# A gather, cumulative sum and product on one core: gathers that convert to fp16 as they land, into 64 slots, in place of a cast on ScalarE

## The chip, the core and the metric

One core of a Trainium2 chip runs the whole program. The metric is device time in microseconds (us) of one execution; the numbers quoted are medians of several executions. A ratio is computed as the mean time of one kernel's fast runs over that of the other's fast runs of the same rounds on the same chip, so it is not quite the ratio of the medians that stand beside it. All times are of the core's own clock, without the host.

Engines: PE is TensorE's matmul, PEld its weight load, DVE is VectorE, ACT is ScalarE, POOL is GpSimd, SP is SyncE. The 16 DMA engines are shared by all queues; q0 carries the gathers, which GpSimd issues, and q1 the stores, which SyncE issues.

## The reference

```python
B, S, N, D = (16, 4096, 2048, 512)      # x: [B, S, D] fp32; indices: sorted, N different ones of S; w: [D, D]
gathered = x[b_idx, indices, :]         # 16 x 2048 rows of 2 KB
cs = np.cumsum(gathered, axis=1)
return np.matmul(cs, w)                 # [16, 2048, 512] fp32
```

In tiles of 128 rows there are T = 256 tiles, 16 to a batch. Each tile is 256 KB of x read and 256 KB of output written, 134 MB in all.

## The kernel before

A tile is gathered, cast to fp16, summed down its rows by four matmuls with a triangle of ones, given the carry of the tile ahead on VectorE, multiplied by w in four matmuls, drained by ScalarE and stored. Two tiles are a pair (R = 2): partition p holds rows 2p and 2p+1 of the pair, so a store writes 4 KB in a row.

```python
NG = 16; FAR = 10; NH = 8; NO = 8       # gather slots, how far casts lead, fp16 pairs, output pairs
g32 = [const.tile([P, R, D], FP32) for i in range(NG // R)]
g16 = [const.tile([P, R, D], FP16) for i in range(NH)]

def gather(t):                          # GpSimd
    g, r = divmod(t, R)
    if t >= NG:
        pool.need(s_c, cast_by[R * (g + 1) - NG - 1])       # the slot has been cast
    ...
    nc.gpsimd.indirect_dma_start(out=g32[g % (NG // R)][:, r, :], in_=x_flat,
        in_offset=bass.IndirectOffsetOnAxis(ap=ap, axis=0), ...).then_inc(s_g[t % NG], 16)

def cast(t, n, first=None):             # ScalarE, in turn with the drains
    ...
    nc.scalar.copy(out=g16[g % NH][:, r : r + n],
                   in_=g32[g % (NG // R)][:, r : r + n]).then_inc(s_c, 1)

def sums(t, u, first=None):             # TensorE
    pe.need(s_c, ...)                   # cast
    ...
def drain(u, first=None):               # ScalarE
    nc.scalar.copy(out=ob[g % NO][:, j], in_=pb[u % NB][:]).then_inc(s_e, 1)

def store(g):                           # SyncE, 512 KB
    nc.sync.dma_start(out=rows.rearrange("(p j) d -> p j d", j=R), in_=ob[g % NO][:])

# order on TensorE: sums lead products by
lead = min(LEAD, 1 + (u + 2) // 4, 1 + (T - 1 - u) // 6)
```

Of the kernel before, what the change touches and what calls it, by code (L numbers as in the profile page):

```python
# [33 lines left out]
def kernel(  # L34
# [19 lines left out]
    FIRST = 2 * R  # L54
    NG = 16
    LEAD = 4
    FAR = 10
    NH = 8
    NA = 4
    NB = 4  # L60
    NC = 4
    NO = 8
    U = NT
    assert U % NG == 0 and U % (R * NO) == 0 and U % NA == 0 and U % (R * NC) == 0 and U % NB == 0
    assert D == 512 and N % (R * P) == 0 and T % P == 0
# [16 lines left out]
    spare = const.tile([P, 1], FP16)  # L82
    g32 = [const.tile([P, R, D], FP32, name=f"g32_{i}") for i in range(NG // R)]
    g16 = [const.tile([P, R, D], FP16, name=f"g16_{i}") for i in range(NH)]
    cst = [const.tile([P, DC, R, P], FP16, name=f"cst{i}") for i in range(NC)]
    ob = [const.tile([P, R, D], FP32, name=f"ob{i}") for i in range(NO)]
    pa = [ps.tile([P, DC, R, Q], FP32, name=f"pa{i}") for i in range(NA)]
# [12 lines left out]
    s_idx = [sem(f"s_idx{k}") for k in range(KI)]  # L100
    s_el = [sem(f"s_el{j}") for j in range(R)]
    s_ol = [sem(f"s_ol{j}") for j in range(R)]
    s_g = [sem(f"s_g{i}") for i in range(NG)]
    s_o = [sem(f"s_o{i}") for i in range(NO)]
# [8 lines left out]

    casts = []
    cast_by = []
    for u in range(T):
        far = min(FAR, 2 + u // 4, 2 + (T - 1 - u) // 4)
        casts.append([])
        while len(cast_by) <= min(u + far, T - 1):
            n = R if far > 4 and len(cast_by) % R == 0 else 1  # L120
            casts[u].append((len(cast_by), n))
            cast_by += [cast_by[-1] + 1 if cast_by else 1] * n

    for u in range(3 * U, T - 2 * U):
        assert casts[u] == [(t + U, n) for t, n in casts[u - U]]

    def gather(t):
        g, r = divmod(t, R)
        if t >= NG:
            pool.need(s_c, cast_by[R * (g + 1) - NG - 1])  # L130
        if t < FIRST:
            pool.need(s_first[g], 16)
            ap = idx_first[:, t, 0:1]
        else:
            pool.need(s_prep, t // P + 1)
            ap = idxg[:, t // P, t % P : t % P + 1]
        nc.gpsimd.indirect_dma_start(  # L137
            out=g32[g % (NG // R)][:, r, :],
            out_offset=None,
            in_=x_flat,  # L140
            in_offset=bass.IndirectOffsetOnAxis(ap=ap, axis=0),
            element_offset=(t // NT) * S * D,
        ).then_inc(s_g[t % NG], 16)


    PLAIN = (0, G - 1)

    def cast(t, n, first=None):
        g, r = divmod(t, R)
        for u in range(t, t + n):  # L150
            act.need(s_g[u % NG], 16 * (u // NG + 1), first)
        nc.scalar.copy(  # L152
            out=g16[g % NH][:, r : r + n], in_=g32[g % (NG // R)][:, r : r + n]
        ).then_inc(s_c, 1)

    def sums(t, u, first=None):
        g, r = divmod(t, R)
        tiles = None if first is None else R * first
        pe.need(s_c, cast_by[t] if first is None else cast_by[2 * U + t] - 2 * U // R, first)
        pe.need(s_d, t - NA + 1, tiles)  # L160
        for c in range(DC):
            if c == 1 and u is not None:
                pe.need(s_e, u - NB + 1, tiles)
            mm = nc.tensor.matmul(  # L164
                out=pa[t % NA][:, c],
                lhsT=g16[g % NH][:, r, c * P : (c + 1) * P],
                rhs=uq[:] if first is None and g in PLAIN else ut[:],
                start=(c == 0),
                stop=(c == DC - 1),
            )  # L170
        mm.then_inc(s_a, 1)
# [28 lines left out]
    def project(u, t, first=None):  # L200
        g, j = divmod(u, R)
        tiles = None if first is None else R * first
        pe.need(s_e, u - NB + 1, tiles)
        pe.need(s_d, u + 1 if first is None and g in PLAIN else R * (g + 1), tiles)
        for c in range(DC):
            if c == 2 and t is not None:
                pe.need(s_d, t - NA + 1, tiles)
            mm = nc.tensor.matmul(  # L208
                out=pb[u % NB][:],
                lhsT=cst[g % NC][:, c, j, :],  # L210
                rhs=w16[:, c, :],
                start=(c == 0),
                stop=(c == DC - 1),
            )
        mm.then_inc(s_b, 1)

    def drain(u, first=None):
        g, j = divmod(u, R)
        act.need(s_b, u + 1, first)
        nc.scalar.copy(out=ob[g % NO][:, j], in_=pb[u % NB][:]).then_inc(s_e, 1)  # L220

    def store(g):
        b, h = divmod(g, GB)
        rows = out[b, h * R * P : (h + 1) * R * P, :]
        if g in PLAIN:
            for j in range(R):
                sp.need(s_e, R * g + j + 1)
                done = s_ol[j] if g else (s_o[0], s_of)[j]
                nc.sync.dma_start(
                    out=rows[j * P : (j + 1) * P, :], in_=ob[g % NO][:, j]  # L230
                ).then_inc(done, 16)
            return
        sp.need(s_e, R * (g + 1))
        nc.sync.dma_start(
            out=rows.rearrange("(p j) d -> p j d", j=R), in_=ob[g % NO][:]
        ).then_inc(s_o[g % NO], 16)

# [15 lines left out]
    for c in range(DC):  # L253
        eng = (nc.sync, nc.scalar)[c % 2]
        eng.dma_start(out=w32[:, c, :], in_=w[c * P : (c + 1) * P, :]).then_inc(s_w[c], 16)
    for g in range(G):
        store(g)
    for g in range(G - NO, G - 1):
        sp.need(s_o[g % NO], 16 * (g // NO + 1))
    for j in range(R):  # L260
        sp.need(s_ol[j], 16)

# [77 lines left out]
    for u in range(T):  # L340
        lead = min(LEAD, 1 + (u + 2) // 4, 1 + (T - 1 - u) // 6)
        first = u if u // R in PLAIN else u // R * R + R - 1
# [6 lines left out]
    tail = order.index((False, T - 2 * U - 1)) + 1  # L349
    step = 2 * U  # L350
    for i in range(head + step, tail):
        assert order[i] == (order[i - step][0], order[i - step][1] + U)

    def run(i, first=None):
        is_sums, t = order[i]
        after = next((v for k, v in order[i + 1 :] if k != is_sums), None)
        if first is not None:
            t -= 2 * U
            after -= 2 * U
        if is_sums:  # L360
# [5 lines left out]
    for i in range(head):  # L366
        run(i)
    with nc.tensor.Fori(2 * U // R, (T - 2 * U) // R, U // R) as first:
        pe.new_pass()
# [11 lines left out]
    def step(u, first=None):  # L381
        if u % R == 0:
            if first is None and u == R * NO:
                act.need(s_of, 16)
            act.need(s_o[u // R % NO], 16 * (u // R // NO), first)
        for t, n in casts[u if first is None else 2 * U + u]:
            cast(t if first is None else t - 2 * U, n, first)
        drain(u, first)
# [40 lines left out]
```

## Time and profile before

| | before |
|---|---|
| time, median of 3 | 353.58 us (353.39 to 354.66) |
| span of its first profile | 447.5 us, granted clock 0.88 |
| GpSimd's gathers | 256, one every 1.25 us at best |
| bytes moved | 135.7 MB |

The page lists groups of instructions with their count, busy time, the mean ns of one, and the idle time ahead of them with what ended most of it. The lines that matter are shown in the prediction. The span of this first profile is 27% longer than the timed runs.

### The profile page before, as it was taken

What the parts mean: (1) busy time and instruction counts of PE and PEld (TensorE: products, weight loads), DVE (VectorE), ACT (ScalarE), POOL (GpSimd) and SP (SyncE); (2) the same over time, 40 slices, a digit from 0 to 9 for tenths busy, and PEclk for the clock granted to TensorE, in tenths of its full rate; (3) what the DMA queues carried; (4) which work ended last, traced back from release to release, by engine and by line L of the source; (5) the groups of instructions that cost most, each with busy time, mean ns of one, the idle gap of its engine ahead of it and who ended that gap; (6) DMA issues with size and microseconds to landing.
All of it is one profiled execution on the core that took longest, in us unless ns stands there. A gap on an engine that the chain in (4) does not pass through costs nothing.

```text
span 447.5 us, 6498 instructions
## 1 busy us (share of the span) xinstructions
PE 340.6 (76%) x2066; PEld 170.5 (38%) x2066; DVE 178.5 (40%) x263; ACT 259.6 (58%) x399; POOL 243.9 (54%) x266
## 2 busy tenths in 40 slices
PE   6354687578858887868788877987588888787995
PEld 2111244244424443424344434444244444344552
DVE  3103344224423454443345433444334444343652
ACT  3212467356636676655567655676456666555984
POOL 6771466575556555655656555655556655555300
PEclk9756789796999698988989889889889889799999
DMA  7874589897899888999989899988898988899974
GB/s 231 255 237 146 187 273 338 312 323 264 311 339 322 298 320 313 343 330 325 326 307 346 313 349 325 327 307 302 334 321 316 333 315 299 313 353 332 336 320 187
DMA packets 40619, 135.69 MB, mean 303 GB/s; under 512 B 6816, under 2 KB 7072, under 8 KB 40608
## 3 DMA queue, kind: packets, MB, share of 16 engines
q0 software_dynamic: 20480, 67.13, 47.3%
q1 hardware_dynamic: 19568, 67.91, 37.7%
q10 hardware_dynamic: 560, 0.53, 0.4%
q8 instruction: 5, 0.08, 0.1%
q14 instruction: 6, 0.05, 0.0%
HBM read 68.42 MB, written 67.11 MB: 303 GB/s over the span
## 4 chain that ended last, share of the span: by engine, by line
PE 70%; issue 12%; another core or an unknown queue 7%; ACT 6%; DVE 3%; DMA 1%; POOL 0%; ACTq 0%; DVEq 0%; SPq 0%
PE pb L208 54%; PE pa L164 16%; ACT g L152 3%; ACT ob L220 3%; DVE cst L196 3%; DMA g<-in_x_dram,idx_first 1%; DMA idx_first<-in_indices_dram 0%; DVE cst L183 0%; POOL g L137 0%; ACTq L26 0%; DVEq L26 0%; ACTq L393 0%; SPq L424 0%; SPq L90 0%
## 5 line engine op out<-in xcount | busy, mean ns | idle before, releaser
L137 POOL DMA_INDIRECT g<-in_x_dram,idxg x252 | 238.4, 946 | 173.1 <-ACT g L152 106.4
L208 PE MATMUL pb<-w,cst 128*128 128x512 f16 x1024 | 297.7, 417 | 44.0 <-issue 21.8
L196 DVE TENSOR_TENSOR cst<-pa,cst 128x512 f16<-128x512 f32 x240 | 166.0, 692 | 241.3 <-PE pa L164 152.4
L220 ACT COPY ob<-pb 128x512 f32<-128x512 f32 x256 | 144.9, 598 | 178.2 <-PE pb L208 118.8
L164 PE MATMUL pa<-ut,g 128*128 128x128 f16 x1008 | 113.1, 233 | 55.0 <-issue 21.3
L208 PEld LDWEIGHTS pb<-w,cst 128*128 128x128 f16 x1024 | 95.2, 106 | 126.2 <-issue 48.0
L152 ACT CAST g<-g 128x1024 f16<-128x1024 f32 (+1 forms) x139 | 138.0, 994 | 0.8 <-DMA g<-in_x_dram,idx_first 0.8
L164 PEld LDWEIGHTS pa<-ut,g 128*128 128x128 f16 x1008 | 81.5, 105 | 137.5 <-issue 45.5
L183 DVE CAST cst<-pa 128x512 f16<-128x512 f32 x16 | 11.0, 688 | 15.6 <-PE pa L164 14.0
L304 PE MATMUL pb<-zeros 128*128 128x512 f16 x16 | 5.7, 521 | 1.5 <-DVE zeros L308 1.5
L137 POOL DMA_INDIRECT g<-in_x_dram,idx_first x4 | 4.0, 994 | 1.6 <-issue 0.9
L304 PEld LDWEIGHTS pb<-zeros 128*128 128x128 f16 x16 | 1.9, 127 | 4.0 <-issue 1.9
L164 PE MATMUL pa<-uq,g 128*128 128x128 f16 x16 | 1.6, 220 | 1.7 <-ACT g L152 0.9
L377 ACT ACT_TABLE_LOAD x1 | 1.3, 1283 | 2.5 <-issue 2.5
L380 ACT CAST w<-w 128x512 f16<-128x512 f32 x2 | 1.1, 614 | 2.7 <-DMA w<-in_w_dram 2.7
L311 DVE CAST idxf<-idx 128x128 f32<-128x128 uint32 x2 | 0.5, 264 | 4.2 <-DMA idx<-in_indices_dram 4.2
L164 PEld LDWEIGHTS pa<-uq,g 128*128 128x128 f16 x16 | 1.0, 97 | 3.0 <-ACT g L152 1.5
L325 DVE CAST w<-w 128x512 f16<-128x512 f32 x2 | 0.8, 424 | 1.2 <-DMA w<-in_w_dram 1.2
L316 PE MATMUL pb<-ident,idxf 128*128 128x128 f32 x2 | 0.8, 376 | 0.5 <-DVE idxf L311 0.5
L316 PEld LDWEIGHTS pb<-ident,idxf 128*128 128x128 f32 x2 | 0.4, 186 | 1.4 <-DVE idxf L311 1.1
L308 DVE MEMSET zeros<- 128x256 uint32 x1 | 0.3, 272 | 1.1 <-SPq L90 1.1
L322 DVE CAST idxg<-pb 128x128 uint32<-128x128 f32 x2 | 0.6, 286 | 0.2 <-issue 0.2
(11 smaller groups left out, 2.1 us busy)
## 6 DMA issues: line engine op xcount, KB each, us to landing
out_dram<-ob SPq DMA_DIRECT2D x126, 512.0 KB
g<-in_x_dram,idxg POOLq DMA_INDIRECT x252
out_dram<-ob SPq DMA_DIRECT2D x4, 256.0 KB, 2.0
w<-in_w_dram ACTq DMA_DIRECT2D x2, 256.0 KB
w<-in_w_dram SPq DMA_DIRECT2D x2, 256.0 KB
idx<-in_indices_dram SPq DMA_DIRECT2D x2, 128.0 KB, 2.7
g<-in_x_dram,idx_first POOLq DMA_INDIRECT x4
idx_first<-in_indices_dram ACTq DMA_DIRECT2D x1, 2.0 KB, 2.1
```

The source lines that it names most:

```text
L137: nc.gpsimd.indirect_dma_start(out=g32[g % (NG // R)][:, r, :], out_offset=None, in_=x_flat, in_offset=bass.IndirectOffsetOnAxis(ap=ap, ax ...
L152: nc.scalar.copy(out=g16[g % NH][:, r : r + n], in_=g32[g % (NG // R)][:, r : r + n]).then_inc(s_c, 1)
L164: mm = nc.tensor.matmul(out=pa[t % NA][:, c], lhsT=g16[g % NH][:, r, c * P : (c + 1) * P], rhs=uq[:] if first is None and g in PLAIN else ...
L183: nc.vector.tensor_copy(out=dst, in_=src).then_inc(s_d, 1)
L196: nc.vector.tensor_tensor(out=dst, in0=src, in1=last, op=mybir.AluOpType.add).then_inc(s_d, 1)
L208: mm = nc.tensor.matmul(out=pb[u % NB][:], lhsT=cst[g % NC][:, c, j, :], rhs=w16[:, c, :], start=(c == 0), stop=(c == DC - 1),)
L220: nc.scalar.copy(out=ob[g % NO][:, j], in_=pb[u % NB][:]).then_inc(s_e, 1)
L304: nc.tensor.matmul(out=pb[NB - 1][:], lhsT=zeros[:, :P], rhs=zeros[:], start=True, stop=True)
L316: nc.tensor.transpose(out=pb[k % NB][:, :P], in_=idxf[:, k, :], identity=ident[:]).then_inc(s_pt, 1)
L325: nc.vector.tensor_copy(out=w16[:, c, :], in_=w32[:, c, :]).then_inc(s_wc, 1)
L377: nc.scalar.copy(out=spare[:], in_=zeros[:, :1])
L380: nc.scalar.copy(out=w16[:, c, :], in_=w32[:, c, :]).then_inc(s_wc, 1)
```

## The change

The intent: ScalarE is freed of 138 us of casts, a slot is no longer held until ScalarE comes round to it, gathers can run far ahead of the sums, and half as many bytes are written into on-chip memory by the gathers. The core of the diff:

```diff
-    NG = 16
+    NG = 64        # slots
+    FLY = 16       # gathers under way at most
+    NS = 32
+    FREE = 8
-    FAR = 10
-    NH = 8
-    NO = 8
+    W = 2          # pairs to a store
+    NO = 4
-    g32 = [const.tile([P, R, D], FP32, name=f"g32_{i}") for i in range(NG // R)]
-    g16 = [const.tile([P, R, D], FP16, name=f"g16_{i}") for i in range(NH)]
+    g16 = [const.tile([P, R, D], FP16, name=f"g16_{i}") for i in range(NG // R)]
     def gather(t):
-        if t >= NG:
-            pool.need(s_c, cast_by[R * (g + 1) - NG - 1])
+        if t % FREE == 0:
+            pool.need(s_a, t + FREE - NG)                                # summed
+        if t >= FLY:
+            pool.need(s_g[(t - FLY) % NS], 16 * ((t - FLY) // NS + 1))   # 16 earlier has landed
         nc.gpsimd.indirect_dma_start(
-            out=g32[g % (NG // R)][:, r, :],
+            out=g16[g % (NG // R)][:, r, :],
-    def cast(t, n, first=None):      # ... gone, and its place in ScalarE's order
     def sums(t, u, first=None):
-        pe.need(s_c, ...)
+        pe.need(s_g[t % NS], ...)
-    def store(g):
+    def store(g, n):                 # n pairs, 1 MB for n = 2
-        lead = min(LEAD, 1 + (u + 2) // 4, 1 + (T - 1 - u) // 6)
+        lead = min(LEAD, 1 if u < 2 else 2 + (u + 4) // 12, (T - 1 - u) // 2)
 # ... cut: semaphores, TensorE's loop of 64 tiles in place of 16, the ends of the stores
```

More of the change, by code (lines that the diff above doesn't have):

```diff
@@ L61 @@
     NC = 4
-    NO = 8
+    W = 2
+    NO = 4
     U = NT
-    assert U % NG == 0 and U % (R * NO) == 0 and U % NA == 0 and U % (R * NC) == 0 and U % NB == 0
+    V = NG
+    assert V % NS == 0 and NS == 16 * R and 2 * U % NS == 0 and (T - 4 * U) % V == 0 and U % (W * R * NO) == 0 and U % NA == 0 and U % (R * NC) == 0 and U % NB == 0
     assert D == 512 and N % (R * P) == 0 and T % P == 0
@@ L82 @@
     spare = const.tile([P, 1], FP16)
-    g32 = [const.tile([P, R, D], FP32, name=f"g32_{i}") for i in range(NG // R)]
-    g16 = [const.tile([P, R, D], FP16, name=f"g16_{i}") for i in range(NH)]
+    g16 = [const.tile([P, R, D], FP16, name=f"g16_{i}") for i in range(NG // R)]
     cst = [const.tile([P, DC, R, P], FP16, name=f"cst{i}") for i in range(NC)]
-    ob = [const.tile([P, R, D], FP32, name=f"ob{i}") for i in range(NO)]
+    ob = [const.tile([P, W, R, D], FP32, name=f"ob{i}") for i in range(NO)]
     pa = [ps.tile([P, DC, R, Q], FP32, name=f"pa{i}") for i in range(NA)]
@@ L100 @@
     s_idx = [sem(f"s_idx{k}") for k in range(KI)]
-    s_el = [sem(f"s_el{j}") for j in range(R)]
-    s_ol = [sem(f"s_ol{j}") for j in range(R)]
-    s_g = [sem(f"s_g{i}") for i in range(NG)]
+    s_ol = sem("s_ol")
+    s_g = [sem(f"s_g{i}") for i in range(NS)]
     s_o = [sem(f"s_o{i}") for i in range(NO)]
@@ L112 @@
     )
-    casts = []
-    cast_by = []
-    for u in range(T):
-        far = min(FAR, 2 + u // 4, 2 + (T - 1 - u) // 4)
-        casts.append([])
-        while len(cast_by) <= min(u + far, T - 1):
-            n = R if far > 4 and len(cast_by) % R == 0 else 1
-            casts[u].append((len(cast_by), n))
-            cast_by += [cast_by[-1] + 1 if cast_by else 1] * n
-    for u in range(3 * U, T - 2 * U):
-        assert casts[u] == [(t + U, n) for t, n in casts[u - U]]
     def gather(t):
         g, r = divmod(t, R)
-        if t >= NG:
-            pool.need(s_c, cast_by[R * (g + 1) - NG - 1])
+        if t % FREE == 0:
+            pool.need(s_a, t + FREE - NG)
+        if t >= FLY:
+            pool.need(s_g[(t - FLY) % NS], 16 * ((t - FLY) // NS + 1))
         if t < FIRST:
@@ L142, in gather @@
             element_offset=(t // NT) * S * D,
-        ).then_inc(s_g[t % NG], 16)
+        ).then_inc(s_g[t % NS], 16)
     PLAIN = (0, G - 1)
-    def cast(t, n, first=None):
-        g, r = divmod(t, R)
-        for u in range(t, t + n):
-            act.need(s_g[u % NG], 16 * (u // NG + 1), first)
-        nc.scalar.copy(
-            out=g16[g % NH][:, r : r + n], in_=g32[g % (NG // R)][:, r : r + n]
-        ).then_inc(s_c, 1)
     def sums(t, u, first=None):
@@ L158, in sums @@
         tiles = None if first is None else R * first
-        pe.need(s_c, cast_by[t] if first is None else cast_by[2 * U + t] - 2 * U // R, first)
-        pe.need(s_d, t - NA + 1, tiles)
+        skip = 0 if first is None else 2 * U
+        pe.need(s_g[t % NS], 16 * (t // NS + 1) - skip // R, first)
+        pe.need(s_d, t - NA + 1 - skip, tiles)
         for c in range(DC):
             if c == 1 and u is not None:
-                pe.need(s_e, u - NB + 1, tiles)
+                pe.need(s_e, u - NB + 1 - skip, tiles)
             mm = nc.tensor.matmul(
                 out=pa[t % NA][:, c],
-                lhsT=g16[g % NH][:, r, c * P : (c + 1) * P],
-                rhs=uq[:] if first is None and g in PLAIN else ut[:],
+                lhsT=g16[g % (NG // R)][:, r, c * P : (c + 1) * P],
+                rhs=uq[:] if g in PLAIN else ut[:],
                 start=(c == 0),
@@ L202, in project @@
         tiles = None if first is None else R * first
-        pe.need(s_e, u - NB + 1, tiles)
-        pe.need(s_d, u + 1 if first is None and g in PLAIN else R * (g + 1), tiles)
+        skip = 0 if first is None else 2 * U
+        pe.need(s_e, u - NB + 1 - skip, tiles)
+        pe.need(s_d, (u + 1 if g in PLAIN else R * (g + 1)) - skip, tiles)
         for c in range(DC):
             if c == 2 and t is not None:
-                pe.need(s_d, t - NA + 1, tiles)
+                pe.need(s_d, t - NA + 1 - skip, tiles)
             mm = nc.tensor.matmul(
@@ L219, in drain @@
         act.need(s_b, u + 1, first)
-        nc.scalar.copy(out=ob[g % NO][:, j], in_=pb[u % NB][:]).then_inc(s_e, 1)
-    def store(g):
+        nc.scalar.copy(out=ob[g // W % NO][:, g % W, j], in_=pb[u % NB][:]).then_inc(s_e, 1)
+    def store(g, n):
         b, h = divmod(g, GB)
-        rows = out[b, h * R * P : (h + 1) * R * P, :]
+        rows = out[b, h * R * P : (h + n) * R * P, :]
+        src = ob[g // W % NO]
         if g in PLAIN:
@@ L227, in store @@
                 sp.need(s_e, R * g + j + 1)
-                done = s_ol[j] if g else (s_o[0], s_of)[j]
+                done = s_ol if g else (s_o[0], s_of)[j]
                 nc.sync.dma_start(
-                    out=rows[j * P : (j + 1) * P, :], in_=ob[g % NO][:, j]
+                    out=rows[j * P : (j + 1) * P, :], in_=src[:, g % W, j]
                 ).then_inc(done, 16)
             return
-        sp.need(s_e, R * (g + 1))
+        sp.need(s_e, R * (g + n))
+        done = {1: s_of, G - W: s_ol}.get(g, s_o[g // W % NO])
         nc.sync.dma_start(
-            out=rows.rearrange("(p j) d -> p j d", j=R), in_=ob[g % NO][:]
-        ).then_inc(s_o[g % NO], 16)
+            out=rows.rearrange("(g p j) d -> p g j d", p=P, j=R),
+            in_=src[:, g % W : g % W + n],
+        ).then_inc(done, 16)
     with nc.allow_non_contiguous_dma(reason="a few indices, one per partition"):
@@ L255 @@
         eng.dma_start(out=w32[:, c, :], in_=w[c * P : (c + 1) * P, :]).then_inc(s_w[c], 16)
-    for g in range(G):
-        store(g)
-    for g in range(G - NO, G - 1):
-        sp.need(s_o[g % NO], 16 * (g // NO + 1))
-    for j in range(R):
-        sp.need(s_ol[j], 16)
+    for g in range(W):
+        store(g, 1)
+    for g in range(W, G - W, W):
+        store(g, W)
+    for g in range(G - W, G):
+        store(g, 1)
+    for i in range(G // W - NO, G // W - 1):
+        sp.need(s_o[i % NO], 16 * (i // NO + 1))
+    sp.need(s_ol, 16 * (R + W - 1))
     nc.gpsimd.memset(ident[:], 1.0).then_inc(s_ut, 1)
@@ L349 @@
     tail = order.index((False, T - 2 * U - 1)) + 1
-    step = 2 * U
+    step = 2 * V
     for i in range(head + step, tail):
-        assert order[i] == (order[i - step][0], order[i - step][1] + U)
+        assert order[i] == (order[i - step][0], order[i - step][1] + V)
     def run(i, first=None):
@@ L356, in run @@
         after = next((v for k, v in order[i + 1 :] if k != is_sums), None)
-        if first is not None:
-            t -= 2 * U
-            after -= 2 * U
         if is_sums:
@@ L367 @@
         run(i)
-    with nc.tensor.Fori(2 * U // R, (T - 2 * U) // R, U // R) as first:
+    with nc.tensor.Fori(2 * U // R, (T - 2 * U) // R, V // R) as first:
         pe.new_pass()
@@ L381, in step @@
     def step(u, first=None):
-        if u % R == 0:
-            if first is None and u == R * NO:
-                act.need(s_of, 16)
-            act.need(s_o[u // R % NO], 16 * (u // R // NO), first)
-        for t, n in casts[u if first is None else 2 * U + u]:
-            cast(t if first is None else t - 2 * U, n, first)
+        if u % (W * R) == 0:
+            if first is None and u == W * R * NO:
+                act.need(s_of, 16 * (R + W - 2))
+            act.need(s_o[u // R // W % NO], 16 * (u // R // W // NO), first)
         drain(u, first)
```

## The prediction

> **What bounds the kernel now.** I read, in this order, the times, the page's engine shares and slices, its DMA queues, its groups, the waits, a table of stretches, and two timelines. The first thing to settle is which run the profile describes: its span is 447.5 us, the three timed runs take 353.39 to 354.66 us. So the profile is 27% longer than what has to be predicted, and I use it for durations, order and ratios, not for the length of waits. These lines of the page carry the case:
>
> ```profile
> span 447.5 us, 6498 instructions
> PE 340.6 (76%) x2066; PEld 170.5 (38%) x2066; DVE 178.5 (40%) x263; ACT 259.6 (58%) x399; POOL 243.9 (54%) x266
> ...
> DMA  7874589897899888999989899988898988899974
> ...
> q0 software_dynamic: 20480, 67.13, 47.3%
> q1 hardware_dynamic: 19568, 67.91, 37.7%
> ...
> HBM read 68.42 MB, written 67.11 MB: 303 GB/s over the span
> ...
> L137 POOL DMA_INDIRECT g<-in_x_dram,idxg x252 | 238.4, 946 | 173.1 <-ACT g L152 106.4
> L208 PE MATMUL pb<-w,cst 128*128 128x512 f16 x1024 | 297.7, 417 | 44.0 <-issue 21.8
> L196 DVE TENSOR_TENSOR cst<-pa,cst 128x512 f16<-128x512 f32 x240 | 166.0, 692 | 241.3 <-PE pa L164 152.4
> L220 ACT COPY ob<-pb 128x512 f32<-128x512 f32 x256 | 144.9, 598 | 178.2 <-PE pb L208 118.8
> ```
>
> No compute engine is above 76%, while the 16 DMA engines sit at mostly eight or nine tenths from the sixth slice to the last but two. The gathers (q0) and the stores (q1) share them about 47 to 38. In the timed runs the same 135.5 MB move in 353.6 us, 383 GB/s over everything, and about 399 GB/s if 14 us of start and end are taken off. That is more than any slice of the profile reaches (353 GB/s at most), so the profile itself slows the transfers.
>
> Beside the DMA engines stands GpSimd's pace of issuing. The timeline of GpSimd shows it where nothing holds it back, and where something does:
>
> ```profile
> 21.15 0.95 POOL L137 DMA_INDIRECT g<-in_x_dram,idxg  x1 [0.30 <-issue]
> 22.40 0.95 POOL L137 DMA_INDIRECT g<-in_x_dram,idxg  x1 [0.30 <-issue]
> 23.65 0.95 POOL L137 DMA_INDIRECT g<-in_x_dram,idxg  x1 [0.30 <-issue]
> ...
> 212.85 0.94 POOL L137 DMA_INDIRECT g<-in_x_dram,idxg  x1 [2.90 <-ACT g L152]
> 214.10 0.95 POOL L137 DMA_INDIRECT g<-in_x_dram,idxg  x1 [0.30 <-issue]
> 215.35 0.94 POOL L137 DMA_INDIRECT g<-in_x_dram,idxg  x1 [0.30 <-issue]
> ```
>
> The start-to-start of two gathers is 1.25 us, from the first ones on, so 256 gathers take at least 320 us. The wait in front of some of them is for ScalarE: a slot of the 16 is free only when ScalarE has cast it, and ScalarE does its casts in turn with the drains, which wait for TensorE. The list of waits puts it at 106.4 us, and shows that nobody waits long for ScalarE's cast otherwise:
>
> ```profile
> DVE cst L196 <- PE pa L164: 152.4, 92, 5.0
> ACT ob L220 <- PE pb L208: 118.8, 70, 4.4
> POOL g L137 <- ACT g L152: 106.4, 38, 6.1
> ...
> PEld pa L164 <- ACT g L152: 29.1, 14, 6.3
> ```
>
> TensorE can do better than either: in the timeline around 213 us one tile's four sums and four products repeat every 1.09 us (starts of the products 212.84, 213.92, 215.01, 216.10), so 256 tiles are 279 us. ScalarE, two drains and a cast of a pair, repeats every 1.90 us in its best stretch (211.53, 213.43, 215.33), 0.95 us per tile. The order of the limits per tile is then: DMA about 1.33 us (353.6 less 14, over 256), GpSimd's issue 1.25, TensorE 1.09, ScalarE 0.95, VectorE 0.69 busy. The margins between the first three are small, and this decides the prediction.
>
> **What the Trainium skill says.** "DMA: Bandwidth & Descriptors", section "Where 436 GB/s comes from", gives a ceiling of 435 GB/s for the 16 ports into the on-chip memory; the section "iDMA fabric" measures one load stream of a lone core at 408.7 GB/s. My 399 GB/s in the timed runs, worked out above, agrees: the kernel is close to what the transfers can do. The same page, "SWDGE vs HWDGE vs iDMA", says that a cast during a DMA is only to be had from GpSimd; the gathers are already issued there, so the change needs no other queue. The page gives no rate for a casting transfer, and the trace before has none, so this is the largest unknown. Its "Rules for kernel authors" ask for at least 1 MiB per DMA; the stores here are 512 KB, yet q1 moves 67.91 MB in 37.7% where q0 takes 47.3% for 67.13 MB, so small stores are not what costs most. "TensorE: Matmul & The Clock Gate", Part 1, says that the clock is halved after an idle window of about 3.4 us; the trace agrees: after the idle of 5 us at 21.4 us the four sums take 0.61 us, and 0.39 us when it has run a while.
>
> **The change part by part.**
> 1. ScalarE's casts go: 117 of 1.064 us and 22 of 0.621 us, 138.0 us. ScalarE is not a limit of its own (0.95 us per tile), so this is worth nothing directly. What it takes off is the 106.4 us of GpSimd waiting for a cast. In the timed runs that wait is much smaller: 353.6 less 3.2 (first gather) less 320 (issue) less a tail of some 10 leaves about 20 us. This is the most that better slots can give: about 6%.
> 2. The gathers convert as they land. They read the same 67 MB and write 33.5 MB in place of 67. If a transfer costs by its source bytes, the DMA work is unchanged; if by the bytes that enter the on-chip memory, the gathers' share halves, and DMA work falls by about 47.3 / 2 of 85.5, 28%. I assume the first, with a somewhat fuller queue.
> 3. 64 slots with at most 16 gathers under way. The number in flight does not rise, but a landed tile no longer takes a place among the 16: in the old scheme a slot is held until the cast, which runs in order behind drains. So the transfer queue stays full through stalls of TensorE. The wait for gather t-16 is asked before every gather; at 1.25 us each, 16 cover 20 us, longer than the 4.9 us from issue to use of the first gather (3.20 to 8.09) on empty queues.
> 4. GpSimd still issues 256 gathers with 128 rows each. I keep 1.25 us: the cast changes neither rows nor instructions.
> 5. Leads and order: sums lead products by up to 4 as before, only the ramps differ; TensorE's instructions are the same 2066. Nothing at 1.09 us per tile.
> 6. Stores: 62 of 1 MB in place of most of the 126 of 512 KB; the bytes are equal. The 16 tiles of output buffer are equal too, but freed by four; a little worth, a little cost: 0.
>
> The sum on the path that I think will bind, GpSimd's: 3.2 (first issue) + 256 x 1.25 = 320, + tail. The tail by row: flight 4.9, sums 0.4, carry 0.7, products 1.0, drain 0.6, store 2.0, together 9.6. That is 333 us. For DMA contention (135.5 MB in 320 us is 423 GB/s, which is above the 399 of now) I add 4: **337 us**, 4.7% less.
>
> **The rivals.**
> Rival A: DMA stays the bound and a converting gather costs by what it reads. For it: nine tenths in the slices, and 399 GB/s near the skill's 408.7. Against it: GpSimd's wait for casts, which says that the queue is not always fed. Then 345 to 353 us, within 2%.
> Rival B: converting is slower than copying, in the DMA engines or in GpSimd's descriptor work. If each gather takes 1.45 us to issue, 256 are 371, and the whole 384 us. Nothing in the trace speaks for it or against it, since there is no converting DMA before; what speaks against it is only that the rest of the change (slots, limits) is laid out around converting gathers, which would be pointless.
> Rival C: the profile inflates GpSimd's 1.25 us as it inflates the span, and the DMA load falls with the bytes written. Then TensorE binds: 10 + 279 + a tail of 6, about 295 to 310 us. For it: the profile's own slowdown; against it: 1.25 us stands even at 5 us into the run, when the DMA queues are nearly empty.
>
> **Range and chances.** Between 333 (issue bound) and 350 (DMA bound) lies most of my belief; below 330 needs C (about 15%), above 361 needs B (about 10%). So 320 to 354 for 8 in 10. Faster by over 2% means below 346.5: 0.66; within 2%: 0.24; slower: 0.10.
>
> **What would show it.** Right: GpSimd's waits for ScalarE gone, gathers at 1.25 us start to start over long stretches, DMA at nine tenths, ScalarE near 150 us busy. Step 2 is wrong if the share of q0 falls well below 47% of the span at equal bytes read, or rises. Step 4 is wrong if a gather's mean is no longer 946 ns. Rival A shows as GpSimd waiting for its own gather of 16 earlier; C as TensorE above 90% with few waits and GpSimd waiting for the sums (a free slot). The prediction fails if a converting gather has another price than a copying one.

## The result

The kernel after takes 354.92 us (354.58 to 355.14, 4 runs) beside 353.59 us for the kernel before: ratio 1.0031, 95% interval 1.0009 to 1.0053. The same within 2%, and if anything a touch slower. Its profile describes the timed runs. These lines of its page answer to those that the prediction shows of before:

```profile
span 353.3 us, 6043 instructions
PE 300.8 (85%) x2066; PEld 150.6 (43%) x2066; DVE 179.2 (51%) x263; ACT 152.4 (43%) x260; POOL 242.1 (69%) x266
...
DMA  7999999999999999999999999999999999999996
...
q0 software_dynamic: 36864, 33.57, 58.8%
q1 hardware_dynamic: 18576, 67.90, 50.1%
...
L127 POOL DMA_INDIRECT g<-in_x_dram,idxg x252 | 236.6, 939 | 79.8 <-issue 70.2
```

ScalarE is down to 152.4 us, most of GpSimd's idle time ends with "issue", that is with no wait that the profile shows, and q0 moves 33.57 MB in place of 67.13, counted as written. But q0's packets take more of the span, not less, the DMA row is nine tenths from the second slice to the last but one, and the two shares add up to over 100%: packets overlap, so these shares are time in flight and not a measure of how full an engine is.

The list of waits gives what GpSimd waited for its gathers (us in total, times, longest):

```profile
POOL g L127 <- issue: 71.1, 233, 0.3
POOL g L127 <- DMA g<-in_x_dram,idxg: 7.1, 14, 1.1
```

It issues at its own pace nearly to the end. What became of the gathers is in the view of the gather line. First its row over the whole span (duration, first and last start), then the time from issue to landing (least, median, most) in the stretches 17 to 60, 60 to 120, 120 to 200, 200 to 280 and 280 to 325 us:

```profile
L127 POOL DMA_INDIRECT g<-in_x_dram,idxg x252: 936/937/1083, 8.4 to 323.5; - x126
...
DMA to landing us min/median/max: 4.2/6.4/8.6
...
DMA to landing us min/median/max: 7.5/9.5/12.1
...
DMA to landing us min/median/max: 11.1/14.0/16.9
...
DMA to landing us min/median/max: 15.9/18.2/20.7
...
DMA to landing us min/median/max: 19.2/20.1/20.9
```

The last gather is issued at 323.5 us, within 2 us of the prediction's pace. But each gather lands later than the one ahead: 6.4 us after issue at first, 20 us in the end, when the limit of 16 under way begins to hold GpSimd back. Gathers are handed over faster than the DMA engines work them off, and 30 us pass between the last issue and the end of the span.

### The profile page after: what moved, and what is told of

Its sections match the earlier page's. It is cut to its first block, busy times and chain, and to the rows that moved or that the text cites. A ratio compares the mean times of both kernels' runs of the same rounds, so it can differ in the third digit from the quotient of the medians.

```text
span 353.3 us, 6043 instructions
## 1 busy us (share of the span) xinstructions
PE 300.8 (85%) x2066; PEld 150.6 (43%) x2066; DVE 179.2 (51%) x263; ACT 152.4 (43%) x260; POOL 242.1 (69%) x266
## 3 DMA queue, kind: packets, MB, share of 16 engines
q0 software_dynamic: 36864, 33.57, 58.8%
## 4 chain that ended last, share of the span: by engine, by line
DMA 43%; POOL 35%; issue 14%; PE 6%; DVE 0%; ACT 0%; SPq 0%; POOLq 0%
DMA g<-in_x_dram,idxg 43%; POOL g L127 35%; PE pb L192 5%; PE pa L147 2%; DMA idx_first<-in_indices_dram 1%; DVE cst L179 0%; ACT ob L204 0%; POOLq L26 0%; SPq L409 0%; SPq L92 0%
## 5 line engine op out<-in xcount | busy, mean ns | idle before, releaser
L192 PE MATMUL pb<-w,cst 128*128 128x512 f16 x1024 | 262.5, 379 | 1.7 <-DVE cst L179 1.4
L204 ACT COPY ob<-pb 128x512 f32<-128x512 f32 x256 | 149.8, 585 | 190.8 <-PE pb L192 190.8
L147 PE MATMUL pa<-ut,g 128*128 128x128 f16 x1008 | 98.3, 220 | 42.7 <-DMA g<-in_x_dram,idxg 41.7
L147 PEld LDWEIGHTS pa<-ut,g 128*128 128x128 f16 x1008 | 68.6, 98 | 126.1 <-DMA g<-in_x_dram,idxg 94.0
L192 PEld LDWEIGHTS pb<-w,cst 128*128 128x128 f16 x1024 | 89.2, 98 | 64.1 <-DVE cst L179 1.7
```

What stands on the lines that cost most here:

```text
L147: mm = nc.tensor.matmul(out=pa[t % NA][:, c], lhsT=g16[g % (NG // R)][:, r, c * P : (c + 1) * P], rhs=uq[:] if g in PLAIN else ut[:], star ...
L192: mm = nc.tensor.matmul(out=pb[u % NB][:], lhsT=cst[g % NC][:, c, j, :], rhs=w16[:, c, :], start=(c == 0), stop=(c == DC - 1),)
L204: nc.scalar.copy(out=ob[g // W % NO][:, g % W, j], in_=pb[u % NB][:]).then_inc(s_e, 1)
```

## The experiments

Eighteen runs were made. Each is compared with the kernel before of its own call. In calls one to three the kernel before takes 352.9 to 354.2 us. In calls four and five it takes 452 us: see the last part.

### Call one: is it the DMA engines, and which bytes count?

**before_again.** No edit; a second profile of the kernel before.

> The kernel before, unchanged, to get a profile of it in the fast state. Theory D (the 16 DMA engines bind both kernels, and a gather costs by the bytes it reads): the time is 353 to 355 us, and if the profile falls in the fast state, GpSimd's gathers come on average every 1.30 to 1.33 us, in place of the 1.243 us of the kernel after, because slots come free late; DMA at nine tenths throughout. Theory G (GpSimd's issue and the wait on its own gathers bind, not the transfers): gathers at 1.25 us without waits here as well. If the profile is again near 447 us, it tells nothing of the timed runs.

Measured: 354.09 us beside 354.18 (ratio 1.0016). From its page, from the view of its gathers over the span, and from its list of waits:

```profile
span 350.9 us, 6498 instructions
...
GB/s 231 246 322 332 313 366 396 403 414 415 415 417 414 415 414 414 415 410 414 413 411 414 406 414 413 409 416 413 411 410 413 411 412 408 413 411 415 415 327 145
...
q0 software_dynamic: 20480, 67.13, 49.8%
q1 hardware_dynamic: 19568, 67.91, 48.0%
...
L137 POOL DMA_INDIRECT g<-in_x_dram,idxg x252: 942/946/958, 8.4 to 322.2; - x126
...
DMA to landing us min/median/max: 3.7/10.1/17.4
...
POOL g L137 <- ACT g L152: 5.8, 19, 0.3
```

This is what the timed runs look like, and it overturns the reading of the first profile. The engines move 406 to 417 GB/s from the ninth slice to the 38th. The gathers are issued until 322.2 us, so GpSimd runs at its own pace here too: the wait of 106.4 us for ScalarE in the first profile is 5.8 us in the state that is timed. This is a profile too, and it reaches 417 GB/s: it was not profiling that slowed the transfers in the first one, as the prediction had it. The expectation of theory D was wrong in this one point (a pace of 1.30 to 1.33 us): 1.25 us, and the gathers land up to 17.4 us after their issue instead. By this trace the kernel before was held by the DMA engines already; the runs below that take bytes away were made in the kernel after.

**plain_gather.** The kernel after without conversion: 64 slots of fp32, and the sums read the upper half of each number as bf16.

```diff
-    ut = const.tile([P, R, Q], FP16)
+    ut = const.tile([P, R, Q], BF16)          # uq too
+    g32 = [const.tile([P, R, D], FP32, name=f"g32_{i}") for i in range(NG // R)]
-    g16 = [const.tile([P, R, D], FP16, name=f"g16_{i}") for i in range(NG // R)]
+    g16 = [g[:].rearrange("p r d -> p (r d)").bitcast(BF16)
+           .rearrange("p (r d w) -> p r d w", r=R, w=2) for g in g32]
-            out=g16[g % (NG // R)][:, r, :],
+            out=g32[g % (NG // R)][:, r, :],
-                lhsT=g16[g % (NG // R)][:, r, c * P : (c + 1) * P],
+                lhsT=g16[g % (NG // R)][:, r, c * P : (c + 1) * P, 1],
```

> The kernel after, but each gather copies fp32 rows as they are into 64 fp32 slots; the sums read the upper halves of the numbers as bf16, so the result is right only to bf16. It takes the conversion away and doubles the bytes written, with bytes read, rows, schedule and issue as they were. Theory D (cost by bytes read, no price for converting): 352 to 358 us, q0 near 58% of 16 engines' span. Theory W (cost by bytes written into the on-chip memory): slower, 370 us or more. Theory C (converting has a price that hides a gain): faster, 335 to 345 us, landing times staying near 5 us.

Measured: 348.6 us, ratio 0.9858 (0.9789 to 0.9926). It lies between D's range and C's: the kernel whose gathers do not convert is faster by some 6 us than the one whose gathers do, although it writes twice the bytes, so converting has a price, as C says and D denies. Theory W is out. The landing times still grow (median 14.0 us in the stretch 280 to 325 us), which C did not expect: the DMA engines bind here as well, only with a higher rate.

**half_gather** and **half_store.** The kernel after with half of the gathers' columns, and with every second store left out; both wrong.

```diff
# half_gather
-            out=g16[g % (NG // R)][:, r, :],
+            out=g16[g % (NG // R)][:, r, :HALF],
-                lhsT=g16[g % (NG // R)][:, r, c * P : (c + 1) * P],
+                lhsT=g16[g % (NG // R)][:, r, c % 2 * P : (c % 2 + 1) * P],
# half_store
         sp.need(s_e, R * (g + n))
+        if n == W and g // W % 2:
+            return
# ... cut: the waits for the stores that are left out
```

> The kernel after, gathers take only the first 256 of 512 columns of each row (wrong result on purpose; the sums use those columns twice). 33.5 MB less are read, the number of rows and packets stays. Theory D: DMA falls below GpSimd's pace, so the last gather is issued at 321 us and lands within 6 us: 329 to 335 us in all, landing times flat near 4 to 5 us. Theory N (cost by the number of row transfers): 350 us or more, as after. Theory G: 353 us, as after.

> The kernel after with every second store of two pairs left out (wrong result on purpose): 33 MB less written, the rest as it was. Theory D: 328 to 335 us with landing times near 5 us, the same as with half gathers, since a saved byte is a saved byte. Theory Q (the gathers' own queue binds, whatever the stores do): landing times still grow to 20 us and the time stays at 350 us or more.

Measured: 338.3 us and 338.44 us, ratios 0.9554 and 0.9552. Their gathers' landing times over the span, half_gather first:

```profile
DMA to landing us min/median/max: 2.7/4.2/7.1
...
DMA to landing us min/median/max: 3.5/5.1/7.4
```

Taking 33 MB away on either side takes the lateness away and gives the same time to 0.2 us; as both end at the same floor, this does not weigh a byte of one against a byte of the other. Theories N, G and Q are out: neither the number of rows, nor GpSimd's waits, nor the gathers' own queue holds the kernel, but the bytes of both queues together. The time reached, 338 us, is 3 us above the range that D expected: what is left is GpSimd's pace and a tail. In half_gather the last gather is issued at 320.5 us and the span ends at 336.5, so the tail is 16 us where the prediction worked out 9.6, though no gather is late there.

### Call two: what has a price, what gains

**same_size_cast.** The slots of plain_gather declared float32r, so that a gather goes through a conversion and still writes all 2 KB.

```diff
-    g32 = [const.tile([P, R, D], FP32, name=f"g32_{i}") for i in range(NG // R)]     # against plain_gather
+    g32 = [const.tile([P, R, D], FP32R, name=f"g32_{i}") for i in range(NG // R)]
```

> The plain-gather variant, but the slots are declared float32r, so each gather goes through a conversion and still writes all 2 KB of a row. Theory K (what costs in the kernel after is converting at all, which also splits the transfer into one packet per row): as slow as the kernel after or slower, 354 to 358 us, with 36864 packets on q0 and landing times that grow past 19 us. Theory S (short writes of 1 KB per row cost): as the plain gathers, 347 to 350 us.

Measured: 356.38 us, ratio 1.0098 (1.0067 to 1.0130). Theory K: it is converting that costs, not the short writes. The q0 lines of plain_gather and of this run (packets, MB, share):

```profile
q0 software_dynamic: 20480, 67.13, 49.7%
```

```profile
q0 software_dynamic: 36864, 67.13, 59.5%
```

For the same bytes there are 36864 packets in place of 20480. 256 gathers on 16 engines make 4096; 20480 is five and 36864 is nine to each, so with 8 rows to an engine a copy carries two rows in a packet and a conversion one (the ninth and the fifth are packets of 4 bytes, 4096 in each trace, which I take for the signal at the end). The steady rate tells the price. The table of stretches for 80 to 320 us, columns from the left: length, busy time and count of PE, PEld, DVE, ACT and POOL, granted clock, DMA share, GB/s; in this order before_again, plain_gather, same_size_cast and the kernel after:

```profile
80.00:320.00 240.00, 216.50 (x1491) 111.13 (x1490) 128.98 (x187) 188.01 (x282) 181.49 (x193) 1.00 1.03 413
...
80.00:320.00 240.00, 223.74 (x1494) 104.06 (x1492) 129.14 (x187) 109.51 (x187) 181.51 (x193) 1.00 1.03 414
...
80.00:320.00 240.00, 209.35 (x1462) 106.50 (x1462) 125.91 (x182) 106.67 (x183) 178.53 (x191) 1.00 1.14 400
...
80.00:320.00 240.00, 209.95 (x1461) 105.67 (x1459) 126.25 (x183) 106.74 (x183) 179.55 (x192) 1.00 1.13 300
```

Copies hold 413 to 414 GB/s under either schedule; converting holds 400. The 300 of the kernel after counts its gathers by the 1 KB written to a row; gathers being about half of the bytes that leave a source, it is about 300 x 4/3 = 400 by source bytes (401 by the trace's packets). Over these 240 us a rate lower by 14 in 414 is 8 us, about what separates plain_gather (348.6) from after (354.9) and from same_size_cast (356.4). Writing 1 KB in place of 2 saves at most the 0.7% between the ratios of the last two, which are of different calls.

**plain_slots16, plain_store_one, plain_casts.** Three parts of the schedule, each taken out of plain_gather by itself.

```diff
# plain_slots16
-    NG = 64
+    NG = 16                        # the loop's length stays 64 tiles
# plain_store_one
-    W = 2
-    NO = 4
+    W = 1
+    NO = 8
# plain_casts: behind each drain; ScalarE's loop is written out
+        act.need(s_dum, u - 3)
+        nc.scalar.copy(out=dum16[:, u % 4], in_=w32[:, 0]).then_inc(s_dum, 1)
```

> The plain-gather variant with 16 slots in place of 64. Theory R (what the new schedule gains is that ScalarE no longer casts and that sums wait for no drain; the slots are not needed, since the gathers land at most 15 us late): 347 to 351 us, as with 64 slots. Theory L (the 64 slots are what gains): back to 353 us or more, with GpSimd waiting for TensorE's sums.

> The plain-gather variant with stores of one pair, 512 KB, in eight buffers as before the change. Expected by all theories: within 0.5% of the plain gathers (347 to 350 us), as the bytes and the 4 KB pieces are the same; 1 to 2 us faster if the coarser stores delay the end or the release of buffers, 2 us or more slower if large stores move better.

> The plain-gather variant with a useless cast of 128x512 behind each drain on ScalarE (256 of 0.62 us, 159 us, a little more than the 138 us that the change removed). Theory R: the drains come later, TensorE waits for them in the ramp, and the time goes back to 351 to 354 us. Theory L: unchanged, 347 to 350 us, ScalarE being at 0.6 + 0.6 us per tile under 1.27.

Measured: 348.55 us (ratio 0.9874, 0.9845 to 0.9903), 350.35 us (0.9927, 0.9899 to 0.9955) and 348.77 us (0.9884, 0.9855 to 0.9912). The 64 slots are not needed, as theory R had it. But ScalarE's load is not what cost either, where R was wrong: 159 us of useless casts change nothing. Stores of two pairs are worth 0.5% (plain_store_one beside plain_slots16, of the same call; just outside the 347 to 350 us expected). So what the new schedule has over the old one, some 1.3%, is not slots and not a freer engine. By the tables of stretches it lies at the two ends: in its first three 20 us plain_gather moves 250, 342 and 396 GB/s and before_again 247, 328 and 364, which is 1 MB or some 2.4 us; and the last of the 40 slices moves 245 against 145.

### Call three: parts of the change in the kernel before, and tries for more

**before_store_two** and **before_leads.** One part of the change alone in the kernel before: stores of two pairs in four buffers (the store function of the diff above); the new ramp of the leads.

```diff
# before_leads
-        lead = min(LEAD, 1 + (u + 2) // 4, 1 + (T - 1 - u) // 6)
+        lead = min(LEAD, 1 if u < 2 else 2 + (u + 4) // 12, (T - 1 - u) // 2)
```

> The kernel before with one part of the change alone: stores of two pairs, 1 MB, in four buffers. With plain gathers going back to 512 KB stores cost 1.8 us. If that is the stores' own effect, this gains 1 to 3 us over before (350 to 352 us); if it only helps in the new schedule, it is within 0.5 us of before.

> The kernel before with the new ramps of the leads of sums over products alone, the casts as they were. If the ramp is what makes the first 60 us move fewer bytes in the kernel before (328 and 364 GB/s in its second and third 20 us, 342 and 396 with plain gathers), this gains 1 to 3 us (350 to 352 us); if the casts in turn with the drains cause it, it is within 0.7 us of before.

Measured: 352.66 us (ratio 0.9977, 0.9929 to 1.0025: not told from no change) and 357.4 us (1.0110, 1.0063 to 1.0157). The stores fall between the two cases expected. The new leads, alone, make the old kernel slower: both expectations for them missed. The rates of its 40 slices, to be read beside those of before_again above, show where:

```profile
GB/s 233 235 316 361 391 376 386 373 383 405 408 414 416 416 416 415 415 416 415 412 411 411 412 410 413 413 405 412 414 412 404 415 399 416 407 414 415 352 146 177
```

The start is as was hoped (354 and 389 GB/s in the second and third 20 us, in place of 328 and 364), though the advantage is lost again by 120 us. The loss is at the end: the last three slices move 352, 146 and 177 where before_again's move 415, 327 and 145. From 300 us on TensorE and its weight loads wait 5.5 and 9.5 us for casts, in before_again 0.2 and 1.2. The edit leaves the ramp of the casts as it was (`far = min(FAR, 2 + u // 4, 2 + (T - 1 - u) // 4)`) while the sums near the end now ask for tiles earlier. So the run tests new leads against an old ramp of casts. The new leads without any cast in the tile's way, with small stores, are plain_store_one at 0.9927; with the casts they are before_leads at 1.0110. By elimination the 1.8% between them would be the price of casts that stand between landing and sum in this order, as the work of casting cost nothing in plain_casts. But the two kernels differ also in slots, in the limit of 16 gathers under way and in TensorE's loop, of which only the slots were taken out; and no run moved the cast's place alone. So the cause of the schedule's gain is argued, not shown.

**plain_one_store** and **plain_rows_four.** Two tries to beat plain_gather: the next store is issued only when the one ahead has landed; four rows to a partition, so that a store writes 8 KB in a row.

```diff
# plain_one_store
+        if n == W and g > W:
+            i = g // W - 1
+            sp.need(s_o[i % NO], 16 * (i // NO + 1))
# plain_rows_four
-    R = 2
+    R = 4
-    NS = 32
+    NS = 64
-    W = 2
+    W = 1
# ... cut: one assertion, the signals of the first and last stores
```

> The plain-gather variant, and each 1 MB store is issued only when the one ahead has landed, so that gathers get more of the DMA engines and stores lag instead. A try to beat both. If the end is idle because gathers land late (14 us after their issue), landing times fall to 5 to 9 us, the last 17 us move over 300 GB/s in place of 250, and the time falls to 341 to 346 us. If one store under way leaves DMA engines idle, or TensorE waits for output buffers, it stays at 347 us or more.

> The plain-gather variant with four rows of a tile group per partition, so that stores write 8 KB in a row in place of 4 KB. If the steady 414 GB/s is set by a price per piece, the rate rises and the time falls by 2 us or more (below 346.5); if it is the ceiling of the bytes, the rate stays at 414 and the time within 2 us of 348.6, rather above, as groups of four tiles wait longer for their products.

Measured: 402.11 us (1.1386) and 353.01 us (0.9977). Neither beats plain_gather. The first is the second case of its expectation (347 us or more), by far; the second is 4 us from the 348.6 it was to stay near. The waits of the first, SyncE's own and ScalarE's, show why:

```profile
SPq L27 <- DMA out_dram<-ob: 344.9, 62, 7.8
```

```profile
ACT ob L206 <- DMA out_dram<-ob: 184.4, 47, 6.2
```

62 waits of 5.6 us for a landing are 345 us: a store of 1 MB by itself does not go faster than that beside the gathers, and ScalarE then stands still for output buffers. With 8 KB in a row the steady rate is 411 GB/s, so 414 is no price of the stores' pieces. That the longer groups cost the 4 us is what was expected and not shown.

### Calls four and five: other chips

**pair_cast, pair_plain, plain_two_stores, after_again, pair_cast_2, pair_plain_2.** The first two gather two neighbouring rows, 4 KB, to an index (wrong data), so that a converting packet carries 4 KB and GpSimd has half the gathers; the third is plain_slots16 with two stores under way; after_again is the kernel after unedited, and the last two repeat the first two.

```diff
# pair_cast, pair_plain
+    x_pair = x.rearrange("b (s r) d -> (b s) (r d)", r=2)
     def gather(t):
+        if r:
+            return
-            out=g16[g % (NG // R)][:, r, :],
+            out=g16[g % (NG // R)][:].rearrange("p r d -> p (r d)"),     # g32 in pair_plain
-            in_=x_flat,
+            in_=x_pair,
# ... cut: the batch's offset, halved; TensorE's wait, for the pair's gather
# plain_two_stores
+        if n == W and g > 2 * W:
+            i = g // W - 2
+            sp.need(s_o[i % NO], 16 * (i // NO + 1))
```

> The kernel after, but each gather fetches two neighbouring rows, 4 KB, per index (wrong data on purpose; the same bytes), so 128 gathers in place of 256: GpSimd needs half its time, and a converting transfer is 4 KB in one packet. Theory P (the price of converting is one per packet): steady rate 410 to 415 GB/s of source bytes (of the counted bytes: 307 to 311) and the same time as pair_plain within 2 us. Theory B (a price per byte converted): steady rate stays at 400 (300 counted), 8 us or more slower than pair_plain.

> The plain-gather variant with two neighbouring rows per index (wrong data on purpose). GpSimd no longer paces the gathers. If the ceiling of the DMA engines is then all that is left: steady 414 GB/s, reached before 40 us in place of 60, and 336 to 343 us. If GpSimd's pace never mattered beside the DMA engines, it stays at 348 us.

> The plain-gather variant with 16 slots, each store of 1 MB issued only when the one two ahead has landed. One under way cost 50 us, since the engines idled between stores. If two keep the engines filled: 345 to 350 us with gathers landing earlier; if a wait per store still leaves gaps, over 352 us and a steady rate below 410 GB/s.

> The kernel after, unchanged, as the reference of this call. On a chip where before takes 353 to 355 us: 354 to 356 us, steady rate 300 GB/s counted, 400 of source bytes. On a chip where before takes near 450 us: if those 100 us are lost because ScalarE's casts and drains hold slots while engines stall, the 64 slots shield it and it stays below 370 us; if the stalls are of TensorE, VectorE and ScalarE themselves, it is 420 us or more, as the plain gathers with 16 slots and two stores under way were (427).

> Gathers of two neighbouring rows per index, converting, one packet per 4 KB (wrong data on purpose). Theory P (price per packet): steady rate within 1% of pair_plain_2's by source bytes (about 310 counted where that one has 414), time within 2 us of it. Theory B (price per byte converted): steady rate 3% below pair_plain_2's and equal to after_again's 300 counted; 6 us or more slower than pair_plain_2.

> The same without conversion (wrong data on purpose). With GpSimd's issue halved, the DMA engines are full before 40 us. On a chip in the usual state, 336 to 345 us if TensorE does not stall in the first 60 us; about 353 us, as in the last call, if saturating the queues that early delays the other engines again.

Measured in call four: the kernel before at 451.94 us, pair_cast 356.05, pair_plain 353.34, plain_two_stores 426.88. In call five, on yet another chip: before 452.68, after 473.54 (ratio 1.0524, 1.0416 to 1.0631), pair_cast_2 356.19, pair_plain_2 353.19.

On these two chips the kernel before takes 28% longer in every run, which is what its very first profile showed (447.5 us). Whether that goes with the chip or with the hour is not shown: each chip was seen in one or two calls. Nothing about the 354 us is concluded from them, and the question of plain_two_stores stays open. What they show is only this: the kernel after is not sheltered by its 64 slots there, it is slower, and its second expectation (420 us or more) held. Two of its waits:

```profile
DVE cst L179 <- remote: 131.2, 25, 21.7
ACT ob L204 <- remote: 89.0, 15, 21.8
```

"Remote" is a wait whose end the profile finds no cause for. VectorE and ScalarE stand for up to 22 us though TensorE has delivered; such waits are absent from the list of before_again and of after on the other chips, and present in the first profile of the kernel before (55.4 and 49.3 us). What delays them I cannot say: open.

The pair runs can be compared with each other. Their stretches from 100 to 260 us in call five, pair_cast_2 first:

```profile
100.00:260.00 160.00, 146.41 (x1044) 78.95 (x1043) 91.30 (x132) 66.98 (x130) 57.14 (x61) 1.00 1.07 309
...
100.00:260.00 160.00, 148.36 (x1058) 80.08 (x1057) 92.08 (x134) 67.50 (x131) 59.17 (x63) 1.00 1.03 419
```

In both GpSimd waits for its gathers to land (some 74 us of these 160), so the DMA engines bind in this stretch. Here 4/3 is too much, since stores and gathers are not equal: 61 gathers of 512 KB in 160 us are 200 GB/s of source bytes and 100 as counted, which leaves 209 for the stores and makes 409; the packets of the trace give 198 + 210 = 408. That is 2.8% below the 419 of pair_plain_2, with as many packets as copying (18432 on q0 in both); with one packet to a row converting cost 3.2 to 3.4%. Call four gives the same rates, 408 and 419. So the steady rate is as theory B has it (a price per byte converted, 3%), and at most a small part of the price goes with the packets. The times differ by 3 us and not by B's 6 or more, as the pair runs are not held by the DMA engines throughout. These two chips are those on which the kernel before takes 452 us; only the rates are used here. That pair_plain comes to 353 and not to 340 us is also not a verdict on GpSimd's pace: TensorE is nearly idle from 20 to 45 us there, while VectorE and ScalarE stand in "remote" waits; both of its expectations missed.

## Why the prediction was wrong

Measured 354.92 us, outside the predicted 320 to 354 and not the 4.7% of gain forecast. By its own steps:

- **What bounds the kernel.** The order of limits was right (DMA about 1.33 us a tile, GpSimd 1.25, TensorE 1.09), and the estimate of 399 GB/s was, if anything, low: 413 in the steady part. It was read and then not obeyed. The reading "the profile itself slows the transfers", on which Rival C also rests, is wrong: before_again's profile reaches 417 GB/s.
- **Part 1, casts worth 20 us.** Wrong. The 20 us between the issue sum and the end were taken for GpSimd waiting for slots. In the fast state GpSimd waits 5.8 us in all for ScalarE and issues its last gather at 322.2 us; the time is lost after that. There before_again takes 28.7 us to the end of the span, of which 16 are the tail as half_gather has it (not 9.6) and some 13 the lateness of the gathers (up to 17.4 us from issue to landing, in place of 3 to 6). The 106.4 us came from a profile of the slow kind, and I scaled it down in place of doubting it.
- **Part 2, converting costs by source bytes.** Half right, and wrong by the sign it set: q0's share rose, to 58.8% beside 49.8 in before_again. Bytes read count and bytes written hardly do (W is out), but converting has a price of its own that I had only as Rival B, in a far larger form: 400 in place of 414 GB/s, 6 to 8 us.
- **Part 3, fuller queue.** Wrong: it was full. With plain gathers 16 slots do as well as 64 (348.55 against 348.6).
- **Part 4, 1.25 us to a gather, last issue at 323 us.** Right: 323.5.
- **Parts 5 and 6.** Leads "nothing" is wrong (1.1% slower alone in the old kernel, at the end, against the old ramp of casts), stores "0" nearly right (0.2% in the old kernel, inside its interval; 0.5% in the new).
- **The term that failed.** "For DMA contention (135.5 MB in 320 us is 423 GB/s, which is above the 399 of now) I add 4": the sum itself says that the engines cannot carry what GpSimd hands over, and the term was mis-sized: the path taken to bind, GpSimd's, was not the one that bound. With the transfers lightened the kernel takes 338 us. With all bytes copied it takes 348.6, 10 us more, and with the gathers converting 354.9, 17 us more: these stand in place of the 4. That 338 is so near the 337 predicted is luck: the 4 us for contention are not in it, and a tail of 16 us in place of 9.6 is. Rival A had the mechanism, and its 345 to 353 us would have held but for the price of converting. Its sign, GpSimd waiting for the gather 16 earlier, hardly showed (7.1 us): the sign to look for was the time from issue to landing, which grows from 6 to 20 us.

Where the gain went: the new schedule does gain, about 5 us (plain_gather 348.6 against 354), and converting takes 6 to 8 us of the DMA engines, which were the bound. The two cancel. That converting is the loss is shown by same_size_cast; which part of the schedule is the gain is not. A version without conversion, plain_gather or plain_slots16, beats before by 1.3 to 1.4%, and by that and the 0.3% of after over before also after; the intervals are clear of 1, but the gain is under 2%. It reads the numbers as bf16 cut short and is less exact.

## What to carry to other kernels

When one resource is near its ceiling in the timed runs, work out what rate the predicted time asks of it, and if that is above what is seen, let that ceiling be the prediction. Where the work runs on an engine with room, moving it into the transfers adds to the resource that has none. And a profile whose span is not the timed one should be taken again before any wait in it is believed: durations and order held, the waits did not.

## What the Trainium skill lacked or had wrong

- "DMA: Bandwidth & Descriptors", section "Where 436 GB/s comes from", says that for transfers between HBM and on-chip memory the HBM side, about 358 GB/s, binds; it gets the figure by dividing a stack's rate by two cores. With this one core in use, gathers and stores together held 413 to 414 GB/s over 240 us, near the same page's 408.7 for one load stream (section "iDMA fabric").
- The same page, "SWDGE vs HWDGE vs iDMA", says where a cast can be had and gives no price. Here rows of 2 KB that convert hold 400 GB/s, whether 1 or 2 KB are written, and copies 414; with 4 KB to an index it is 408 and 419.
- The same section gives packets of at most 4096 B preferably. It lacks that a converting row of 2 KB travels alone: 36864 packets against 20480 for the same rows.
- The same page's "Rules for kernel authors" ask for 1 MiB per DMA. Going from 512 KB to 1 MB was worth 0.2% (not told from nothing) in one schedule and 0.5% in another, with the engines full in both.
- No page has the two levels seen here: one program, 353 to 354 us on the chips of calls one to three and 452 us on those of calls four and five, in every run.
